# Output projection of an attention layer as seven products of 512-wide blocks in place of eight

## Chip, core and metric

The kernel runs on one core of a Trainium2 chip. The metric is the device time in microseconds (us) of one execution, as the median of several. The engines are TensorE (PE for matmuls, PEld for the loads of their stationary operand), VectorE (DVE), ScalarE (ACT), GpSimd (POOL) and SyncE (SP), which only issues DMAs here.

## What is computed

One layer over a sequence of 1024 rows of width 1024: adaLN, an input projection, two groups of eight attention heads of width 64, each head gated by SiLU, an output projection, a gated residual and a layer norm.

```python
y_fox = _from_heads(fox_out) * silu(fg)          # forgetting attention
y_sb  = _from_heads(sb_out) * silu(sg)           # stick-breaking attention
y = concatenate([y_fox, y_sb], -1) @ w_out       # (1024 x 1024) @ (1024 x 1024)
x = layer_norm(ALPHA * x + gate * y, ln_g, ln_b)
```

All is in float32. The kernel splits both operands of a product into a rounded part ("hi", type fp32r) and the rest ("lo") and sums three products, hi x hi, lo x hi and hi x lo, in PSUM.

## The kernel before

Heads are handled in eight pairs: pairs 0 to 3 are stick-breaking, 4 to 7 forgetting (the layout puts the rows of w_out in that order). A unit is one head of a pair and 128 queries (`order`, L983); 128 units run one after another. For a unit TensorE makes the scores (`att_scores`, L414), ACT, DVE and POOL make the weights; two units later TensorE transposes them (`att_transpose`, L465), and when two neighbours are there it multiplies with the values (`att_pv`, L486): the product is gated on POOL (L514) and stored to DRAM in `y_dr` (L522), that of pair 7 split on the spot into `y7h` and `y7l` (L519, L520).

The order on TensorE is written out by hand (`manual_schedule`, L806); the order on the other engines and in the DMA queues comes from the framework's scheduler, which may put their work well ahead of its place in the text. Between the units `fill` (L978) lets TensorE do steps of the projections of later pairs (`gen_m`, L294; `gen_v`, L342). Their weights come through two raw buffers (`raw_tile`, L113) and are split by `fetch_w` (L119) into a ring of five pairs of tiles (`ring_w`, L116).

Beside the projections of pairs 4 to 7 runs `gen_split_out` (L825): sixteen times it fetches 128 x 512 of w_out, multiplies by the gate (L123), splits (L125, L126) and stores both parts to `wo_dr` (L830, L831), and then lets SPACE = 5 steps pass. During the last projection (`gen_last_g`, L944) the places of u are set free one by one, and `load_wo` (L818) fills them with the split w_out, 512 KB each.

From the fifth unit of pair 7 on, `TAIL` (L973) asks for 2, later 4 and 8 steps of the output projection a unit; the rest follows after the last unit. A step is `o_step` (L871): three matmuls (L882 to L884) of 128 rows (t), one pair, and 512 columns. Rows are taken in `OUT_ORDER`, late ones first, as pair 7 finishes them; `load_y` (L855) fetches and splits the other pairs' values for a row tile on POOL (L862, L863). `o_half` (L888) adds the residual (L897) and takes statistics (L899); after the second half DVE applies gain and bias (L910, L912), read from SBUF (`lngb`) at first, and from PSUM (`ps_gain`, `ps_bias`) after `ln_to_psum`.

## Time and profile before

| | us |
|---|---|
| runs, median of 3 (lowest, highest) | 685.15 (684.91, 685.39) |
| span of the profiled execution | 683.5 |
| matmuls end, from the span's start | 676.7 |
| DMA moved over the span | 81.60 MB |

The profiled execution is listed by its span, from the first to the last instruction; what lies around the span is not shown, and the median stands 1.65 us above it. Times in rows count from the span's start. A matmul's row shows when it starts and how long it is in the pipeline; neighbours overlap, so the distance between starts is what one costs. Idle time of an engine that is not the bottleneck costs nothing.

### The profile page before, as it was taken

Reading aid. Unit: us, or ns where it says so; the run is one execution under the profiler, and the core shown is the slowest. Engines: PE = TensorE matmul, PEld = TensorE weight load, DVE = VectorE, ACT = ScalarE, POOL = GpSimd, SP = SyncE. Lnnn points to the kernel's source line nnn. Section 1 sums busy time; section 2 is a strip of 40 time slices with the busy share of each in tenths; the row PEclk is TensorE's granted clock in tenths of the full one; section 3 lists DMA queues with packets and bytes.
Section 4 is the critical chain, followed back from the end, with each engine's and each line's share of the span. In section 5 each row is a group of like instructions: output and inputs, shape, how many; then the busy total and the mean of one; then the engine's idle time right before and its main releaser. Section 6 shows DMA issues by size and latency. Waiting matters only on the chain.

```text
span 683.5 us, 11770 instructions
## 1 busy us (share of the span) xinstructions
PE 667.2 (98%) x4021; PEld 587.2 (86%) x4021; DVE 450.6 (66%) x914; ACT 382.0 (56%) x861; POOL 427.7 (63%) x558
## 2 busy tenths in 40 slices
PE   5999999999999999999999999999999999999995
PEld 4789898888998888889988888899988889888885
DVE  6785368867666667676675665765566677774645
ACT  5668357856567666566675564655565667531000
POOL 5558977756348566556388896877584364665411
PEclk9999999999999999999999999999999999999999
DMA  9966231112102121122144563453341298143301
GB/s 338 410 236 233 82 105 44 41 29 60 29 9 86 27 57 54 37 55 55 55 131 136 172 176 121 143 166 129 101 150 40 72 327 318 58 162 118 123 31 62
DMA packets 45036, 81.60 MB, mean 119 GB/s; under 512 B 5232, under 2 KB 18864, under 8 KB 44976
## 3 DMA queue, kind: packets, MB, share of 16 engines
q1 hardware_dynamic: 43536, 76.63, 33.8%
q10 hardware_dynamic: 1440, 4.21, 2.2%
q8 instruction: 32, 0.52, 0.3%
q14 instruction: 28, 0.23, 0.1%
HBM read 60.34 MB, written 16.29 MB: 112 GB/s over the span
## 4 chain that ended last, share of the span: by engine, by line
PE 94%; DMA 3%; DVE 2%; ACT 0%; issue 0%; POOL 0%; DVEq 0%
PE m L270 10%; PE m L272 10%; PE m L271 10%; PE pv L493 10%; PE T L478 9%; PE S L428 5%; PE S L427 5%; PE o L884 4%; PE o L882 4%; PE o L883 4%; PE v L327 4%; PE v L328 4%; PE v L329 4%; DMA raws<-in_w_qkg_dram 2%; PE st_late L589 1%; PE st_q L589 1%
## 5 line engine op out<-in xcount | busy, mean ns | idle before, releaser
L270 PE MATMUL m<-uh,whi 128*128 128x512 f32 x304 | 126.4, 416 | 0.0
L272 PE MATMUL m<-uh,wlo 128*128 128x512 f32 x304 | 119.7, 394 | 0.0
L271 PE MATMUL m<-ul,whi 128*128 128x512 f32 x304 | 119.7, 394 | 0.0
L481 DVE TENSOR_TENSOR pt<-T,pt 128x512 fp32r<-128x512 f32 (+2 forms) x192 | 100.5, 550 | 17.5 <-ACT pt L480 16.5
L461 POOL TENSOR_TENSOR be<-be,kp 128x127 f32<-128x127 f32 (+3 forms) x64 | 77.2, 1207 | 33.1 <-DVE kp L457 23.5
L480 ACT CAST pt<-T 128x512 fp32r<-128x512 f32 (+2 forms) x192 | 85.8, 480 | 16.1 <-PE T L478 12.5
L453 DVE TENSOR_TENSOR_SCAN kp<-kp,floor 128x512 f32<-128x512 f32 (+2 forms) x64 | 65.2, 1018 | 31.2 <-ACT kp L447 30.1
L493 PEld LDWEIGHTS pv<-pt,v 128*128 128x128 f32 (+1 forms) x640 | 77.1, 163 | 4.4 <-DVE pt L481 0.7
L493 PE MATMUL pv<-pt,v 128*128 128x256 f32 (+3 forms) x640 | 80.4, 271 | 0.5 <-DVE pt L481 0.5
L442 POOL TENSOR_SCALAR a<-a,l 128x1024 f32<-128x1024 f32 (+3 forms) x64 | 48.1, 751 | 40.3 <-DVE l L441 26.7
L272 PEld LDWEIGHTS m<-uh,wlo 128*128 128x128 f32 x304 | 57.1, 188 | 13.6
L440 ACT ACTIVATE a<-a,nm 128x1024 f32<-128x1024 f32 (+3 forms) x64 | 49.8, 778 | 33.8 <-DVE nm L434 32.7
L427 PE MATMUL S<-k,q 128*128 128x512 f32 (+5 forms) x192 | 66.5, 348 | 0.2 <-DVE nm L434 0.2
L428 PE MATMUL S<-kl,qz 128*128 128x512 f32 (+5 forms) x192 | 65.5, 342 | 0.0
L270 PEld LDWEIGHTS m<-uh,whi 128*128 128x128 f32 x304 | 57.3, 188 | 8.5 <-DVE kl L258 0.2
L271 PEld LDWEIGHTS m<-ul,whi 128*128 128x128 f32 x304 | 57.4, 189 | 8.0
L434 DVE CUSTOM_DVE_ANT_0 a<-S,fb 128x1024 f32<-128x1024 f32 (+3 forms) x64 | 48.3, 755 | 20.1 <-PE S L428 9.3
L514 POOL TENSOR_TENSOR ty<-ty,sg 64x256 f32<-64x256 f32 x64 | 47.5, 742 | 22.3 <-DVE ty L513 11.1
L447 ACT ACTIVATE kp<-S 128x128 f32<-128x128 f32 (+3 forms) x64 | 41.7, 652 | 31.6 <-PE S L428 29.4
L327 PE MATMUL v<-whi_v,uh 128*128 128x256 f32 (+1 forms) x192 | 56.0, 292 | 0.0
L405 ACT CAST qz<-q 64x128 fp32r<-64x128 f32 x128 | 37.4, 295 | 33.2 <-PE S L428 31.8
L328 PE MATMUL v<-whi_v,ul 128*128 128x256 f32 (+1 forms) x192 | 54.2, 282 | 0.0
(285 smaller groups left out, 1593.6 us busy)
## 6 DMA issues: line engine op xcount, KB each, us to landing
raw<-in_w_qkg_dram SPq DMA_DIRECT2D x38, 256.0 KB, 2.9
wss<-in_w_ss_dram SPq DMA_DIRECT2D x16, 512.0 KB, 8.4
x<-in_x_dram SPq DMA_DIRECT2D x8, 512.0 KB, 6.9
k<-k SPq DMA_DIRECT2D x32, 128.0 KB, 2.3
wg<-in_w_gate_dram SPq DMA_DIRECT2D x8, 512.0 KB, 4.9
raw_o<-in_w_out_dram SPq DMA_DIRECT2D x16, 256.0 KB, 2.8
fb<-f_dr ACTq DMA_DIRECT2D x8, 512.0 KB, 4.3
wo_dr<-whi_o SPq DMA_DIRECT2D x16, 256.0 KB, 2.5
```

Of the source, the lines that this page charges most:

```text
L270: nc.tensor.matmul(acc, hi[:, c], u_hi[kt][:, s], start=(kt == 0), stop=False)
L271: nc.tensor.matmul(acc, hi[:, c], u_lo[kt][:, s], start=False, stop=False)
L272: nc.tensor.matmul(acc, lo[:, c], u_hi[kt][:, s], start=False, stop=(kt == NB - 1))
L327: nc.tensor.matmul(acc[:, :n], u_hi[kt][:, ts_], hi[:, s], start=(kt == 0), stop=False)
L328: nc.tensor.matmul(acc[:, :n], u_lo[kt][:, ts_], hi[:, s], start=False, stop=False)
L427: nc.tensor.matmul(S[:, s, :w], qst[p][h][:, qs], kst[p][h][:, ks], start=True, stop=False)
L428: nc.tensor.matmul(S[:, s, :w], z, klo[p][:, ks], start=False, stop=True)
L453: scan = nc.vector.tensor_tensor_scan(rv, rv, floor[0][:, 512 - n:][:, ::-1], initial=0.0, op0=ALU.mult, op1=ALU.max)
L461: nc.gpsimd.tensor_tensor(be[:, :ke - 1], be[:, :ke - 1], kp[:, 1:ke], op=ALU.mult)
L480: nc.scalar.copy(hi[:, :n, qo:qo + P], t3)
L481: nc.vector.tensor_tensor(lo[:, :n, qo:qo + P], t3, hi.bitcast(F32)[:, :n, qo:qo + P], op=ALU.subtract)
L493: nc.tensor.matmul(acc[:m, q0:256], vt[p][:, kb, h * P:h * P + m], pt[:, kb % 4, q0:], start=start, stop=stop)
```

## The change

Y (rows x heads) and W (heads x columns) are cut into four blocks of 512 x 512. Y's A11, A12 are rows 0 to 511 (LOW) of pairs 0 to 3 and 4 to 7, A21 and A22 are rows 512 to 1023 (HIGH); B11, B12, B21, B22 likewise. In place of eight block products there are seven: S1 = A21 + A22, S2 = S1 - A11, S3 = A11 - A21, S4 = A12 - S2; T1 = B12 - B11, T2 = B22 - T1, T3 = B22 - B12, T4 = B21 - T2 (the code stores it so); p1 = A11 B11, p2 = A12 B21, p3 = S4 B22, p4 = A22 T4, p5 = S1 T1, p6 = S2 T2, p7 = S3 T3. The four result blocks are sums of these products, which DVE adds. `gen_split_out` makes and stores all seven weight blocks, with a partial sum held in one of the two raw buffers. All heads' values go to `y_dr`, and `PREP` and the generators load them back in blocks of 512 rows, add on POOL, and split. The lower four row tiles get p7, p6, p4 and p5 and are finished by `lower_done` (ACT, POOL); the upper four are started with p1, p6 and p5, and finished with p2 and p3 in `gen_last`. `y_a11`, `y_a22` and `y_s1` load one block and split it as the others do; `upper_done` is the old `o_half`'s end, `load_rows` and `load_upper` fetch x.

```diff
-    SPACE = 5
+    SPACE = 3
...
-    wo_dr = dr.tile([2, NPAIR, P, D], F32, tag="wo_dr", name="wo_dr")
+    OPS = ("B11", "T3", "T2", "T4", "T1", "B21", "B22")
+    wo_dr = dr.tile([len(OPS), 2, 2, P, D], F32, tag="wo_dr", name="wo_dr")
+    s_dr = dr.tile([2, 4, P, 512], F32, tag="s_dr", name="s_dr")
...
-        if p == NPAIR - 1:
...
-            nc.scalar.copy(yh[r, qs], yt[r, :])
-            nc.gpsimd.tensor_tensor(yl[r, qs], yt[r, :], yh.bitcast(F32)[r, qs], op=ALU.subtract)
-        else:
-            nc.sync.dma_start(y_dr[p, r, qs], yt[r, :])
+        nc.sync.dma_start(y_dr[p, r, qs], yt[r, :])
...
+    def load_op(name, jp, tags):
...
+            nc.sync.dma_start(t.bitcast(F32), wo_dr[o, x_, jp])
...
     def gen_split_out():
-        for pr in range(NPAIR):
-            for h in range(2):
-                s = slice(h * 512, h * 512 + 512)
-                hi, lo = fetch_w(f"o{pr}_{h}", w_out[pr * P:(pr + 1) * P, s], 512, gate[:, s])
-                nc.sync.dma_start(wo_dr[0, pr, :, s], hi.bitcast(F32)[:, :512])
-                nc.sync.dma_start(wo_dr[1, pr, :, s], lo.bitcast(F32)[:, :512])
-                for _ in range(SPACE):
-                    yield
+        def fetch(pr, h, key):
+            s = slice(h * 512, h * 512 + 512)
+            raw = raw_tile(f"raw_o{key}")[:, :512]
+            nc.sync.dma_start(raw, w_out[pr * P:(pr + 1) * P, s])
+            nc.gpsimd.tensor_tensor(raw, raw, gate[:, s], op=ALU.mult)
+            return raw
+        def store(name, j, raw):
+            hi, lo = (t[:, :512] for t in ring_w(f"o{name}{j}"))
+            nc.scalar.copy(hi, raw)
+            nc.gpsimd.tensor_tensor(lo, raw, hi.bitcast(F32), op=ALU.subtract)
+            at = slice(j % 2 * 512, j % 2 * 512 + 512)
+            for x_, t in enumerate((hi, lo)):
+                nc.sync.dma_start(wo_dr[OPS.index(name), x_, j // 2, :, at], t.bitcast(F32))
+        def less(out, a, b):
+            nc.vector.tensor_tensor(out, a, b, op=ALU.subtract)
+            return out
...
+        for j in range(4):
+            cur = fetch(j, 0, f"a{j}")
+            store("B11", j, cur)
+            yield from pause()
+            new = fetch(j, 1, f"b{j}")
+            cur = less(new, new, cur)
+            store("T1", j, cur)
+            yield from pause()
+            new = fetch(4 + j, 1, f"c{j}")
+            store("B22", j, new)
+            cur = less(new, new, cur)
+            store("T2", j, cur)
+            yield from pause()
+            yield from pause()
+            new = fetch(j, 0, f"d{j}")
+            store("T3", j, less(new, cur, new))
+            yield from pause()
+            new = fetch(4 + j, 0, f"e{j}")
+            store("B21", j, new)
+            store("T4", j, less(new, new, cur))
+            yield from pause()
+            yield from pause()
...
+        lgb[0] = [att_tile(f"ln_{x_}") for x_ in "gb"]
+        nc.sync.dma_start(lgb[0][0], ln_g.to_broadcast([P, D]))
+        nc.sync.dma_start(lgb[0][1], ln_b.to_broadcast([P, D]))
...
+    def raw_pair(key, home=None):
+        turns[0] += 1
+        if home is None and turns[0] % 2:
+            home = gate
+        if home is not None:
+            return home[:, LOW], home[:, HIGH]
+        return [raw_tile(f"y{x_}_{key}")[:, :512] for x_ in "ab"]
+    def y_home(name, j):
+        jp, at = j // 2, slice(j % 2 * 512, j % 2 * 512 + 512)
+        if name in ("A11", "A22"):
+            if (name, jp) not in yop:
+                yop[name, jp] = sb.tile([P, 4, 512], F32R, tag="v", bufs=3, name=f"y{name}_{jp}")
+            yop[name, j, "t"] = [yop[name, jp][:, 2 * (j % 2) + x_, :] for x_ in range(2)]
+        elif name in ("S2", "S4"):
+            yop[name, j, "t"] = [t[:, :512] for t in ring_w(f"{name}_{j}")]
         else:
+            tags = {"S3": ("u4", "v4", "u5", "v5"), "S1": ("u4", "v4", "u5", "v5"),
+                    "A12": ("q", "q", "k", "k")}[name][2 * jp:2 * jp + 2]
+            if (name, jp) not in yop:
+                yop[name, jp] = [big(t, 4 if t in "qk" else 1, f"y{name}_{jp}_{x_}", F32R)
+                                 for x_, t in enumerate(tags)]
+            yop[name, j, "t"] = [t[:, at] for t in yop[name, jp]]
+        return yop[name, j, "t"]
+    def y_split(name, j, raw):
+        hi, lo = y_home(name, j)
+        nc.scalar.copy(hi, raw)
+        nc.gpsimd.tensor_tensor(lo, raw, hi.bitcast(F32), op=ALU.subtract)
+    def y_less(out, a, b):
+        nc.gpsimd.tensor_tensor(out, a, b, op=ALU.subtract)
...
+    def y_s3(j):
+        a, b = raw_pair(f"S3{j}")
+        nc.sync.dma_start(a, y_dr[j, :, LOW])
+        nc.sync.dma_start(b, y_dr[j, :, HIGH])
+        y_less(b, a, b)
+        y_split("S3", j, b)
+    def y_s2(j):
+        a, b = raw_pair(f"S2{j}")
+        nc.sync.dma_start(a, y_dr[j, :, HIGH])
+        nc.sync.dma_start(b, y_dr[4 + j, :, HIGH])
+        nc.gpsimd.tensor_tensor(b, a, b, op=ALU.add)
+        nc.sync.dma_start(s_dr[0, j], b)
+        nc.sync.dma_start(a, y_dr[j, :, LOW])
+        y_less(a, b, a)
+        nc.sync.dma_start(s_dr[1, j], a)
+        y_split("S2", j, a)
...
+    def y_s4(j):
+        home = (lambda: big("sg", 2, "y_c0"), lambda: big("kl", 2, "y_c1"), lambda: gate, lambda: None)[j]()
+        a, b = raw_pair(f"S4{j}", home) if home is not None else [raw_tile(f"y{x_}_S4{j}")[:, :512] for x_ in "ab"]
+        nc.sync.dma_start(b, s_dr[1, j])
+        for c in (slice(256, 512), slice(0, 256)) if j == 3 else (LOW,):
+            nc.sync.dma_start(a[:, c], y_dr[4 + j, :, c])
+            (hi, lo), (hi4, lo4) = yop["A12", j, "t"], yop["S4", j, "t"]
+            nc.scalar.copy(hi[:, c], a[:, c])
+            nc.gpsimd.tensor_tensor(lo[:, c], a[:, c], hi.bitcast(F32)[:, c], op=ALU.subtract)
+            y_less(b[:, c], a[:, c], b[:, c])
+            nc.scalar.copy(hi4[:, c], b[:, c])
+            nc.gpsimd.tensor_tensor(lo4[:, c], b[:, c], hi4.bitcast(F32)[:, c], op=ALU.subtract)
+    def block_step(acc, yname, wname, t, j, a=0, b=512):
+        yh, yl = (v[:, t * P:(t + 1) * P] for v in yop[yname, j, "t"])
+        hi, lo = w_of(wname, j, a, b)
+        acc = acc[:, :b - a]
+        nc.tensor.matmul(acc, yh, hi, start=j == 0, stop=False)
+        nc.tensor.matmul(acc, yl, hi, start=False, stop=False)
+        nc.tensor.matmul(acc, yh, lo, start=False, stop=j == 3)
...
+    def add_to(r, s, acc):
+        nc.vector.tensor_tensor(r[:, s], r[:, s], acc, op=ALU.add)
...
+    def lower_done(t):
+        r, row = lower[t], 4 + t
...
+        sums, rs, squares = small("sums"), small("rs"), [pv_tile(f"sq_{x_}_{row}", x_) for x_ in range(2)]
...
+        nc.scalar.activation(r, r, AF.Identity, accum_out=sums[:, 0:1])
+        nc.gpsimd.tensor_scalar(mv[:, 0:1], sums[:, 0:1], -1.0 / D, 1.0, op0=ALU.mult, op1=ALU.mult)
+        for x_, s in enumerate((LOW, HIGH)):
+            nc.scalar.activation(squares[x_], r[:, s], AF.Square, bias=mv[:, 0:1],
+                                 accum_out=(sums[:, 1:2], mv[:, 1:2])[x_])
+        nc.gpsimd.tensor_tensor(rs[:, 0:1], sums[:, 1:2], mv[:, 1:2], op=ALU.add)
+        nc.gpsimd.tensor_scalar(rs[:, 0:1], rs[:, 0:1], 1.0 / D, EPS, op0=ALU.mult, op1=ALU.add)
+        nc.gpsimd.tensor_tensor(rs[:, 0:1], rs[:, 0:1], mhalf, op=ALU.pow)
+        nc.gpsimd.tensor_tensor(rs[:, 1:2], mv[:, 0:1], rs[:, 0:1], op=ALU.mult)
+        nc.scalar.activation(r, r, AF.Identity, scale=rs[:, 0:1], bias=rs[:, 1:2])
+        for s in (LOW, HIGH):
+            nc.gpsimd.tensor_tensor(r[:, s], r[:, s], lgb[0][0][:, s], op=ALU.mult)
+            nc.vector.tensor_tensor(r[:, s], r[:, s], lgb[0][1][:, s], op=ALU.add)
+            nc.sync.dma_start(out[row * P:(row + 1) * P, s], r[:, s])
...
+    def gen_first_half():
+        for p0 in (0, 2):
+            ts = (p0, p0 + 1)
+            accs = {t: acc_tile(f"p1_{t}") for t in ts}
+            for jp in range(2):
+                for t in ts:
+                    for j in (2 * jp, 2 * jp + 1):
+                        block_step(accs[t], "A11", "B11", t, j)
+                        yield
+                    if jp:
+                        if t % 2 == 0:
+                            c1[t // 2] = big(("sg", "kl")[t // 2], 2, f"c1_{t // 2}")
+                        nc.scalar.copy(c1[t // 2][:, t % 2 * 512:][:, :512], accs[t])
+            if p0 == 2:
+                for jp in range(2):
+                    load_op("T4", jp, (("u0", "v0"), ("u1", "v1"))[jp])
+                for j in range(4):
+                    y_a22(j)
+            for t in ts:
+                acc = acc_tile(f"p7_{t}")
+                for j in range(4):
+                    block_step(acc, "S3", "T3", t, j)
+                    yield
+                for s in (LOW, HIGH):
+                    nc.vector.scalar_tensor_tensor(lower[t][:, s], lower[t][:, s], ALPHA, acc,
+                                                   op0=ALU.mult, op1=ALU.add)
+        for jp in range(2):
+            load_op("T1", jp, (("u2", "v2"), ("u3", "v3"))[jp])
+        for j in range(4):
+            y_s1(j)
+    def product(acc, yname, wname, t):
+        for j in range(4):
+            block_step(acc, yname, wname, t, j)
+            yield
+    def gen_second_half():
+        u2 = [pt_tile(x_, f"u2_{x_}", F32, [P, 2, 512]) for x_ in range(2)]
+        for p0 in (0, 2):
+            ts = (p0, p0 + 1)
+            for t in ts:
+                acc = acc_tile(f"p6_{t}")
+                yield from product(acc, "S2", "T2", t)
+                nc.vector.tensor_tensor(u2[t // 2][:, t % 2], c1[t // 2][:, t % 2 * 512:][:, :512], acc, op=ALU.add)
+                for s in (LOW, HIGH):
+                    add_to(lower[t], s, u2[t // 2][:, t % 2])
+            if p0 == 2:
+                for jp in range(2):
+                    load_op("B22", jp, (("u6", "v6"), ("u7", "v7"))[jp])
+                for j in range(4):
+                    y_home("A12", j)
+                    y_home("S4", j)
+                    y_s4(j)
+            for t in ts:
+                acc = acc_tile(f"p4_{t}")
+                yield from product(acc, "A22", "T4", t)
+                add_to(lower[t], LOW, acc)
+            if p0 == 0:
+                load_ln()
+                for t in range(3, -1, -1):
+                    load_upper(t)
+                for jp in range(2):
+                    load_op("B21", jp, ("pth", "ptl"))
+            for t in ts:
+                acc = acc_tile(f"p5_{t}")
+                yield from product(acc, "S1", "T1", t)
+                add_to(lower[t], HIGH, acc)
+                for s, part in ((LOW, c1[t // 2][:, t % 2 * 512:][:, :512]), (HIGH, u2[t // 2][:, t % 2])):
+                    nc.vector.scalar_tensor_tensor(upper[t][:, s], upper[t][:, s], ALPHA, part,
+                                                   op0=ALU.mult, op1=ALU.add)
+                add_to(upper[t], HIGH, acc)
+                lower_done(t)
+        ln_to_psum()
+    def gen_last():
+        for t in range(3, -1, -1):
+            final = t == 0
+            acc = acc_tile(f"p2_{t}")
+            for j in range(4):
+                block_step(acc, "A12", "B21", t, j)
                 yield
+            add_to(upper[t], LOW, acc)
+            groups = ((0, 256), (256, 512)) if final else ((0, 512),)
+            row_stats(upper[t], t, 0, LOW, 1 + len(groups))
...
+            for g, (a, b) in enumerate(groups):
+                acc = acc_tile(f"p3_{t}_{a}")
+                for j in range(4):
+                    block_step(acc, "S4", "B22", t, j, a=a, b=b)
+                    yield
+                s = slice(512 + a, 512 + b)
+                add_to(upper[t], s, acc[:, :b - a])
+                row_stats(upper[t], t, 1 + g, s)
+            upper_done(t)
...
-            load_wo(kt)
+            home = (("B11", 0), ("B11", 1), ("T3", 0), ("T3", 1), None, None, ("T2", 0), ("T2", 1))[kt]
+            if home:
+                load_op(*home, (f"u{kt}", f"v{kt}"))
...
-    YLOAD = (6, 9, 12, 14, 16)
+    PREP = {-4: (y_a11, 0), -2: (y_a11, 1), 2: (y_a11, 2), 3: (y_a11, 3), 4: (y_s3, 0), 5: (y_s3, 1),
+            6: (y_s3, 2), 7: (y_s3, 3), 8: (y_s2, 0), 9: (y_s2, 1), 10: (y_s2, 2), 12: (y_s2, 3)}
...
-    tail = chain([gen_out_first(6), gen_out_last(6)] + [gen_out(t) for t in OUT_ORDER[1:]])
+    tail = chain([gen_first_half(), gen_second_half(), gen_last()])
...
-        if k == LAST:
-            load_y(6)
-            load_ln()
-        for i, d in enumerate(YLOAD):
-            if k == LAST + d:
-                load_y(OUT_ORDER[i + 1])
-    for t in OUT_ORDER[1 + len(YLOAD):]:
-        load_y(t)
-    ln_to_psum()
+        if k - LAST in PREP:
+            prepare, j = PREP[k - LAST]
+            prepare(j)
+        if 3 <= k - LAST < 7:
+            load_rows(k - LAST - 3)
```

155 lines of the change are left out of this document (64 added, 91 removed).

## The prediction, made before the changed kernel ran

> **What bounds the kernel now.** I read the page first (busy shares, then the chain that ended last), and then the table of windows, to see which engine has room in which stage.
>
> ```profile
> span 683.5 us, 11770 instructions
> PE 667.2 (98%) x4021; PEld 587.2 (86%) x4021; DVE 450.6 (66%) x914; ACT 382.0 (56%) x861; POOL 427.7 (63%) x558
> PE 94%; DMA 3%; DVE 2%; ACT 0%; issue 0%; POOL 0%; DVEq 0%
> ```
>
> The chain is TensorE for 94% of the span: taking matmuls away shortens the kernel, as long as what feeds TensorE keeps up. The 63% of POOL is a mean over very different stages. The windows hold PE, PEld, DVE, ACT and POOL busy, then the clock, the DMA share and GB/s.
>
> ```profile
> core 0: us, PE busy (x) PEld busy (x) DVE busy (x) ACT busy (x) POOL busy (x), PEclk, DMA share, GB/s
> 340.00:490.00 150.00, 150.00 (x962) 135.11 (x961) 94.45 (x241) 85.69 (x212) 119.23 (x131) 1.00 0.45 139
> 490.00:560.00 70.00, 69.74 (x399) 59.69 (x397) 46.75 (x122) 42.01 (x103) 40.44 (x50) 1.00 0.44 140
> 560.00:634.50 74.50, 74.50 (x414) 64.02 (x412) 51.72 (x122) 34.18 (x84) 43.02 (x56) 1.00 0.49 176
> 634.50:676.70 42.20, 42.15 (x205) 34.88 (x203) 21.62 (x36) 0.00 (x0) 8.80 (x15) 1.00 0.19 68
> 676.70:683.50 6.80, 0.00 (x0) 0.00 (x0) 3.70 (x8) 0.55 (x1) 1.43 (x3) 0.85 0.21 77
> ```
>
> TensorE is full in every stage up to 676.7. POOL is at 119 of 150 us (79%) where the output weights are split (340 to 490), at 58% beside the last head pair, and nearly idle after 634.5. The change loads just these three places.
>
> **The matmuls removed.** A matmul row lasts 395 ns but overlaps its neighbours, so a matmul costs its distance to the next.
>
> ```profile
> 628.94 0.40 PE L882 MATMUL o<-woh,whi_y 128*128 128x512 f32 x1
> ...
> 634.97 0.39 PE L884 MATMUL o<-wol,whi_y 128*128 128x512 f32 x1
> ```
>
> Between these two starts lie 26 matmuls of 512 columns: 6.03 / 26 = 0.232 us each. Before, the projection is 8 row tiles x 8 pairs x 2 halves x 3 = 384 such matmuls (one half cut in two). After, it is 7 products x 4 row tiles x 4 blocks x 3 = 336. 48 x 0.232 = **11.1 us less**. The closing chain after the last matmul (6.8 us above) keeps its instructions. The loop over the units asks for the same counts of steps (3 x 0.232 = 0.696 us each) as before, 68 in all. Before, 68 are left after it, 16 of them of half width: 52 x 0.696 + 16 x 0.348 = 41.8 us ahead of 676.5, so it ends near 634.7, and it would after the change too, with 48 left. p2 of row tile 3, the first to need A12, then starts at 634.7 + 12 x 0.696 = 643, and p3, which needs S4, asks for its last block near 648.
>
> **The weight sums beside the projections.**
>
> ```profile
> L123 POOL TENSOR_TENSOR raw_o<-raw_o,gate 128x512 f32<-128x512 f32 x15 | 19.5, 1298 | 9.6 <-DMA raw_o<-in_w_out_dram 9.4
> L126 POOL TENSOR_TENSOR wlo_o<-raw_o,whi_o 128x512 fp32r<-128x512 f32 x15 | 19.5, 1298 | 0.7
> L125 POOL TENSOR_SCALAR whi_o<-raw_o 128x512 fp32r<-128x512 f32 x16 | 9.9, 618 | 0.9 <-PE m L271 0.7
> L480 ACT CAST pt<-T 128x512 fp32r<-128x512 f32 x29 | 16.5, 586 | 2.0 <-PE T L478 1.5
> L126 POOL TENSOR_TENSOR wlo<-raw,whi 128x512 fp32r<-128x512 f32 x13 | 16.8, 1295 | 1.3 <-DMA wo_dr<-wlo_o 0.8
> L126 POOL TENSOR_TENSOR wlo_v<-raw_v,whi_v 128x512 fp32r<-128x512 f32 x4 | 5.2, 1296 | 0.3
> raw_o<-in_w_out_dram SPq DMA_DIRECT2D x16, 256.0 KB, 2.8
> L121 SPq DMA_DIRECT2D raw_o<-in_w_out_dram x16: 328/333/577, 314.6 to 475.5; - x16
> L126 POOL TENSOR_TENSOR wlo_o<-raw_o,whi_o x16: 1283/1296/1316, 346.1 to 490.0; 128x512 fp32r<-128x512 f32 x16
> ```
>
> POOL before: 16 x (1.298 + 0.618 + 1.298) = 51.4 us. After: 20 gate products and 28 low parts, 48 x 1.298 = 62.3: 10.9 more, with which the stage stands at 130 of 150 (87%). ACT gains 28 casts, 16.4 us by L480's 586 ns; DVE 16 subtractions, 12 us by 0.75 (L912 below). None of these engines gets full. What is tight is the two raw buffers: a partial sum holds one of them through 15 of the 21 pauses of a round, and the other serves everything else. By these rows four fetches of a round keep it for 4.9 + 6.7 + 6.7 + 8.6 = 27 us, 108 over four rounds; the projections' 17 fetches (13 + 4 above) of 2.8 + 0.62 + 1.30 = 4.7 us add 80. That is 188 us, against the stage's 314.6 to 490 = 175 us x 1.29 (both free for 6 of 21) = 226. It fits at 83%. I take 1 us; the ends are 0 (the projections' matmuls hide it) and 13 us (188 on one buffer alone). The added stores and loads go down SP's queue, with DMA at 0.45 here: no cost.
>
> **The row-side blocks: POOL at the end.** Rows of 560 to 683.5:
>
> ```profile
> L863 POOL TENSOR_TENSOR wlo_y<-yr,whi_y 128x512 fp32r<-128x512 f32 x6 | 7.8, 1301 | 0.4
> L863 POOL TENSOR_TENSOR wlo_y<-yr,whi_y 128x384 fp32r<-128x384 f32 x6 | 6.1, 1017 | 0.5
> L520 POOL TENSOR_TENSOR y7l<-ty,y7h 64x256 fp32r<-64x256 f32 x8 | 5.9, 737 | 2.3 <-ACT y7h L519 2.1
> L176 POOL TENSOR_TENSOR rs_b<-rs_b,mhalf 128x1 f32<-128x1 f32 x7 | 5.4, 771 | 0.6
> L862 POOL TENSOR_SCALAR whi_y<-yr 128x512 fp32r<-128x512 f32 x6 | 3.7, 620 | 1.7 <-PE o L884 0.9 <-POOL ty L514 0.5
> L862 POOL TENSOR_SCALAR whi_y<-yr 128x384 fp32r<-128x384 f32 x6 | 3.1, 515 | 18.7 <-PE o L884 18.7
> L175 POOL TENSOR_SCALAR rs_b<-mv_b 128x1 f32<-128x1 f32 x7 | 2.8, 407 | 13.9 <-DVE mv_b L170 13.6
> ```
>
> Of the 43.0 us of POOL in 560 to 634.5, about 31 go (the y splits 20.7, y7l 5.9, statistics some 4), and 12 of attention stay. Added: 28 low parts and 16 sums, 44 x 1.30 = 57.2, of which two are ready before 560: 54.6. Further lower_done, per row 5 small operations (an estimate of 2.8 us from L175 and L176) and 2 x 1.30: 5.4, two rows of them ahead of 648: 10.8. Together 12 + 54.6 + 10.8 = 77 us in the 88 from 560 to 648. And there is a further claim, on the port:
>
> ```profile
> L910 DVE SCALAR_TENSOR_TENSOR r<-r,mv_b,lngb 128x512 f32<-128x512 f32 x8 | 6.7, 880 | 0.1
> L912 DVE SCALAR_TENSOR_TENSOR r<-r,rs_b,lngb 128x512 f32<-128x512 f32 x8 | 5.9, 747 | 1.5 <-POOL rs_b L176 1.4
> L910 DVE SCALAR_TENSOR_TENSOR r<-r,mv_b,ps_gain 128x512 f32<-128x512 f32 x7 | 5.0, 744 | 0.1
> L176 POOL TENSOR_TENSOR rs_b<-mv_b,mhalf 128x1 f32<-128x1 f32 x1 | 0.6, 569 | 5.2 <-DVE mv_b L170 5.2
> ```
>
> The same DVE operation takes 880 ns with both operands in SBUF and 744 with the gain in PSUM; POOL's power of 128x1 takes 771 beside the first and 569 beside the second. So the two hold each other up. The change gives DVE 20 such operations ahead of 648 (8 sums of u2 into lower rows, 8 starts of upper rows, 4 bias sums). I price POOL's standstill at 0.75 each, 15 us, for POOL is seldom idle there: 92 us in 88. The ends are 0 and 15. The Trainium skill (SBUF — State Buffer, "SBUF: two separate sides") says that a DVE operation with two SBUF inputs and a POOL operation that reads SBUF exclude each other for a whole instruction; the rows above point that way. By that rule the excess stands; without it POOL would have 11 us to spare.
>
> POOL is thus 4 us over if nothing gives way; 4.1 us of the second row's close (2 x 1.30 + 2 x 0.75) may run behind S4. Between 0 and 4, and with idle moments before landings, I take **3 us** of wait, at p2 and p3 of row tile 3; in TensorE's queue every later product stands behind it. lower_done also squares into the banks of pv and fl, so the loop's last pv product waits for row 5's squares: a sum over the row (some 1.1 us), one small POOL operation and a square, about 3 us after p5, beside which p6 of row tile 2 runs for 2.8. I take 0; if POOL is late, it counts among the same 3 us.
>
> **DVE in the last stage.**
>
> ```profile
> L899 DVE BATCH_NORM_STATS2 st_b<-r 128x6 f32<-128x512 f32 x15 | 10.4, 693 | 0.4
> L897 DVE SCALAR_TENSOR_TENSOR r<-xr,o 128x512 f32<-128x512 f32 x15 | 10.2, 686 | 22.6 <-PE o L884 22.5
> ```
>
> Before, a row tile costs DVE 2 x (0.69 + 0.69) + 4 x 0.74 + 0.21 = 5.9 us under 48 x 0.232 = 11.1 us of matmuls; L897 waits 22.5 us for TensorE in all. In gen_last the same work of upper_done stands beside only 24 x 0.232 = 5.6 us. DVE falls behind by 0.3 us a row, starts late by what lower_done's bias sums leave, and the last half finds up to 3 us of the row before in DVE's queue: **1.5 us**, ends 0 and 4.
>
> **The sum** for the profiled execution: 683.5 - 11.1 + 1 + 3 + 1.5 = 677.9. The median of the runs, 685.15, lies 1.65 us above that span; with the same added, **679.5 us**.
>
> **The rivals.**
>
> 1. Everything is hidden, and only the matmuls count: 685.15 - 11.1 = 674.0; without the port's hold-up, but with the 1 and 1.5 above, 676.6. For it: in the plain count POOL has 11 us to spare. Against it: the 880 and 771 ns. Chance 0.20 (up to 677).
>
> 2. The forecast, 677 to 683.8: 0.45.
>
> 3. The waits eat the gain, within 0.2% of before (about what a measurement of this kernel tells from no change): 683.8 to 686.5, when they come to 10 to 12 us: 0.10.
>
> 4. **Slower: the two staging pairs (gate and the raw buffers) that carry S3, S2, A22 and S1 in turn become the chain.**
>
> ```profile
> yr<-y_dr SPq DMA_DIRECT2D x8, 256.0 KB, 3.4
> wol<-wo_dr SPq DMA_DIRECT2D x8, 512.0 KB, 7.7
> 559.73 0.78 PE L493 MATMUL pv<-pt,v 128*128 128x256 f32 x4
> 628.53 0.57 PE L493 MATMUL pv<-pt,v 128*128 128x256 f32 x4
> ```
>
> A11's second half can be split only when pair 6's values are free, after its last pv product at 559.7. From about 564 on each pair carries two blocks of every kind: S3 2 x (2.9 + 1.3 + 0.6 + 1.3), S2 2 x (2.9 + 1.3 + 2.9 + 1.3 + 0.6 + 1.3), A22 and S1 2 x 4.8 each (landing 2.9, an estimate between 2.8 and 3.4): 12.2 + 20.6 + 9.6 + 9.6 = 52 us, so S1 is ready at 616. p5 wants it at 620, twelve steps (8.4 us) ahead of the last pv product at 628.5. Each of a pair's 14 POOL operations may have to wait for what POOL is at: with 0.65 (half of 1.30) 9 us, and S1 comes at 625. With two landings like the 7.7 us under load, 9.6 more, it comes at 634.6, 14.6 us late, in which the 3 us of p2 are contained: 685.15 - 11.1 + 1 + 14.6 + 1.5 = 691.2; with one, 686.4. It decides from 8.6 us of lateness on (11.1 - 1 - 1.5). For it: POOL's 77 to 92 us in 88, and 2.1 MB each of T4, T1, B21 and B22 beside it on the DMA queues. Against it: every block but pair 7's is in DRAM early, and landings of 256 KB took 3.4 us here, the 7.7 us being those of 512 KB in a burst. Chance 0.25.
>
> One row bears on the price of long waits:
>
> ```profile
> 679.00:681.00 2.00, 0.00 (x0) 0.00 (x0) 1.57 (x4) 0.52 (x1) 0.59 (x1) 1.00 0.16 62
> 682.00:683.50 1.50, 0.00 (x0) 0.00 (x0) 0.00 (x0) 0.00 (x0) 0.00 (x0) 0.50 0.04 11
> ```
>
> The granted clock is still 1.00 until 681, 4 us after the last matmul (TensorE is idle from 676.7), and 0.50 from 682: short waits keep it. The Trainium skill (TensorE: Matmul & The Clock Gate, "What's actually happening") puts the window of idleness that halves the clock at about 3.4 us; one wait in a single piece beyond that would by the page cost up to another 3.4 us, which would put the fourth case near 694.
>
> **How the numbers follow.** Faster by over 0.2%: 0.20 + 0.45 = 0.65; same 0.10; slower 0.25. The range, 674.0 to 691.0, goes from the bare count of matmuls to the fourth case's price; some 0.1 lies above (the 13 us of the raw buffers, more long landings), little below, since nothing here removes more than the 48 matmuls. The forecast's own range is 677 to 683.8.
>
> **What would show it.** 336 matmuls' worth of rows in block_step at the same pitch of 0.23; PE idle of some 3 us at p2 and p3 of row tile 3, released by POOL; POOL at 85% or more from 560 to 648; bias and u2 sums on DVE over 0.75 us beside POOL; PE full from 340 to 490. Wrong, if TensorE waits in the projections for whi (raw buffers), at p5 for S1, or nowhere.

## The result and the profile after

The change makes the kernel **slower**: 765.09 us, median of 4 runs (764.07 to 768.32), against 685.27 us (684.91 to 685.41) of the kernel before beside it. The ratio is 1.1175, 95% interval 1.1151 to 1.1199. The forecast was 679.5.

The page of the kernel after: span, busy time of each engine, and the chain that ended last, by engine.

```profile
span 764.3 us, 11991 instructions
PE 684.5 (90%) x3961; PEld 590.3 (77%) x3961; DVE 476.1 (62%) x942; ACT 425.6 (56%) x943; POOL 479.6 (63%) x585
PE 60%; DMA 14%; POOL 12%; DVE 7%; issue 5%; ACT 2%; SPq 0%; POOLq 0%; ACTq 0%; DVEq 0%
```

TensorE was the chain for 94%, now for 60%. POOL is busy for 63% of the span as before, and yet has taken 12% of the chain: that points to its place in a row of waits more than to its load. TensorE's largest waits in the kernel after, from 340 us to the end (total, times, longest):

```profile
PE m L272 <- POOL whi L127: 14.3, 4, 4.8
PE p L978 <- ACT yA L922: 12.8, 2, 10.2
PE v L329 <- POOL whi_v L127: 8.3, 4, 2.8
PE p L978 <- DVE r L993: 6.8, 4, 4.0
PE T L480 <- DVE pt L483: 3.7, 3, 2.2
PE S L429 <- DVE nm L436: 3.3, 3, 1.5
PE m L274 <- POOL wlo L128: 3.3, 3, 2.5
```

The same view of the kernel before has one line for 340 to 683.5:

```profile
PE S L427 <- DVE nm L434: 0.2, 1, 0.2
```

Two groups stand out: projections (m, v) that wait for their split weights, and products of the output projection (p) that wait for a row block (yA) or for VectorE (r). The windows (columns as in the prediction) cut the run where pair 7's last projection (`gen_last_g`) begins, at 600.8 after and 548.4 before; first after, then before:

```profile
340.00:600.90 260.90, 225.98 (x1302) 194.69 (x1301) 142.89 (x358) 136.12 (x326) 164.89 (x168) 0.93 0.41 133
600.90:764.30 163.40, 127.13 (x615) 102.01 (x614) 100.78 (x197) 69.91 (x155) 99.97 (x112) 0.91 0.62 218
```

```profile
340.00:548.40 208.40, 208.14 (x1300) 185.27 (x1299) 132.90 (x341) 121.12 (x295) 151.29 (x170) 1.00 0.42 129
548.40:628.80 80.40, 80.40 (x448) 68.91 (x447) 57.13 (x138) 39.99 (x100) 46.25 (x61) 1.00 0.57 204
628.80:676.40 47.60, 47.60 (x232) 39.49 (x229) 24.50 (x39) 0.77 (x2) 13.96 (x21) 1.00 0.20 70
```

The first stage, that of the weight sums, is 600.8 - 548.4 = **52.4 us later**: TensorE is idle for 34.9 us (0.3 before), and its 1300 matmuls are busy for 17.8 us longer (225.98 against 208.14), at the lower clock. The last stage takes 163.4 us where it took 683.5 - 548.4 = 135.1: **28.3 more**, and 39.4 more than the 124.0 that 11.1 us of removed matmuls would have left. The granted clock has fallen to 0.93 and 0.91.

### The profile page after: what moved, and what is told of

Its sections match the earlier page's. It is cut to its first block, busy times and chain, and to the rows that moved or that the text cites. A ratio compares the mean times of both kernels' runs of the same rounds, so it can differ in the third digit from the quotient of the medians.

```text
span 764.3 us, 11991 instructions
## 1 busy us (share of the span) xinstructions
PE 684.5 (90%) x3961; PEld 590.3 (77%) x3961; DVE 476.1 (62%) x942; ACT 425.6 (56%) x943; POOL 479.6 (63%) x585
## 4 chain that ended last, share of the span: by engine, by line
PE 60%; DMA 14%; POOL 12%; DVE 7%; issue 5%; ACT 2%; SPq 0%; POOLq 0%; ACTq 0%; DVEq 0%
PE m L274 7%; PE m L272 7%; PE m L273 7%; PE pv L493 7%; PE T L480 6%; PE v L331 3%; PE v L329 3%; PE S L430 3%; PE v L330 3%; PE S L429 3%; DMA raws<-in_w_qkg_dram 2%; DMA gate<-s_dr 2%; POOL wlo L128 2%; DMA yb_S<-y_dr 2%; DMA raw<-in_w_qkg_dram 1%
## 5 line engine op out<-in xcount | busy, mean ns | idle before, releaser
L272 PE MATMUL m<-uh,whi 128*128 128x512 f32 x304 | 128.8, 424 | 14.3 <-POOL whi L127 14.3
L274 PE MATMUL m<-uh,wlo 128*128 128x512 f32 x304 | 122.3, 402 | 3.5 <-POOL wlo L128 3.3
L273 PE MATMUL m<-ul,whi 128*128 128x512 f32 x304 | 121.5, 400 | 0.0
L482 ACT CAST pt<-T 128x512 fp32r<-128x512 f32 (+2 forms) x192 | 85.8, 480 | 17.9 <-PE T L480 14.5
L493 PEld LDWEIGHTS pv<-pt,v 128*128 128x128 f32 (+1 forms) x640 | 80.9, 170 | 6.0 <-DVE pt L483 1.1
L493 PE MATMUL pv<-pt,v 128*128 128x256 f32 (+3 forms) x640 | 84.4, 279 | 1.0 <-DVE pt L483 0.8
L444 POOL TENSOR_SCALAR a<-a,l 128x1024 f32<-128x1024 f32 (+3 forms) x64 | 50.4, 788 | 38.6 <-DVE l L443 29.6
L513 DVE TENSOR_TENSOR ty<-pv,ty 64x256 f32<-64x256 f32 x64 | 26.9, 420 | 62.6 <-ACT ty L512 51.6
L331 PE MATMUL v<-wlo_v,uh 128*128 128x256 f32 (+1 forms) x192 | 55.5, 289 | 2.8 <-POOL wlo_v L128 2.8
```

Source lines behind the costliest of these rows:

```text
L272: nc.tensor.matmul(acc, hi[:, c], u_hi[kt][:, s], start=(kt == 0), stop=False)
L273: nc.tensor.matmul(acc, hi[:, c], u_lo[kt][:, s], start=False, stop=False)
L274: nc.tensor.matmul(acc, lo[:, c], u_hi[kt][:, s], start=False, stop=(kt == NB - 1))
L331: nc.tensor.matmul(acc[:, :n], u_hi[kt][:, ts_], lo[:, s], start=False, stop=(kt == NB - 1))
L482: nc.scalar.copy(hi[:, :n, qo:qo + P], t3)
L493: nc.tensor.matmul(acc[:m, q0:256], vt[p][:, kb, h * P:h * P + m], pt[:, kb % 4, q0:], start=start, stop=stop)
```

## The experiments

Each kernel was run once, beside the kernel before (685.05 to 686.16 us on the same chips). The kernel after spreads over 4.3 us in its four runs, so differences of a few us between single times mean little; the start of `gen_last_g` and the rest behind it are read from each kernel's trace. They scatter too: the nine kernels with the same weight sums (after, e4, t_a, t_b, t_c, f1, f2, g1, g2) start between 599.6 and 604.6, and the nine with the same work in the last stage (after, e1, e5, f3, f4, g3, h1, h2, h3) take 161.6 to 165.5 for the rest. Steps under 4 or 5 us below are therefore not clear of the scatter by themselves; they are read beside TensorE's waits in the traces.

| kernel | us | gen_last_g starts | rest of the span |
|---|---|---|---|
| before | 685.27 | 548.4 | 135.1 |
| after | 765.09 | 600.8 | 163.4 |
| e3_before_sums | 735.58 | 598.8 | 135.1 |
| e1_nohold | 732.72 | 565.8 | 165.2 |
| e2_before_hold | 688.18 | 551.4 | 135.1 |
| f4_keep | 753.94 | 589.9 | 162.3 |
| e5_noless | 726.19 | 559.9 | 164.6 |
| f3_16 | 722.96 | 557.1 | 164.1 |
| g3_fetch16 | 720.17 | 556.8 | 161.6 |
| h1_even | 723.37 | 556.1 | 165.5 |
| h2_80 | 720.74 | 554.5 | 164.4 |
| h3_cast | 716.24 | 549.1 | 165.1 |
| e4_order | 768.18 | 602.3 | 164.2 |
| t_c_port | 771.85 | 604.6 | 165.5 |
| t_b_noload | 754.22 | 599.6 | 152.9 |
| t_a_nosums | 749.90 | 602.7 | 145.5 |
| f1_both | 747.19 | 600.5 | 144.9 |
| f2_nolow | 742.95 | 600.6 | 140.3 |
| g1_dve | 738.86 | 602.3 | 134.8 |
| g2_noclose | 735.44 | 599.7 | 134.0 |

Some expectations count these starts from a zero up to 0.6 us apart, and say 11.2, 8.3 and 5.9 for what is 11.5, 8.7 and 6.1 here.

### The two stages apart

e3_before_sums is the kernel before with the new `gen_split_out` alone; its projection loads whatever blocks lie there.

```diff
-        nc.sync.dma_start(hi.bitcast(F32), wo_dr[0, pr])
+        nc.sync.dma_start(hi.bitcast(F32), wo_dr[pr % 7, 0, pr // 4])
```

> The kernel before with the changed gen_split_out (seven blocks, sums held) and the old projection of eight products, whose weights are read from the seven blocks, so the projection is not the reference's. If the weight sums cost what the traces suggest (gen_last_g 51.8 us late) and nothing else of the change does so ahead of pair 7: 685 + 50 = 735. If the late start comes from the row-side work that is put ahead of its place (y_a11 and y_s3 beside the projections): 685 to 700.

It came to 735.58, 50.4 us late at `gen_last_g` and with the old rest of 135.1. The weight sums lose some 50 us by themselves, with nothing of the seven products in the kernel.

### The held raw buffer

```diff
-            cur = less(new, new, cur)
+            cur = less(new, new, new)      # e1, at each of the four sums
```

e1_nohold subtracts a block from itself, so no partial sum lives across the pauses; the work is the same.

> The changed kernel with every subtraction of weight blocks taken within one buffer (new - new in place of new - cur), so that no partial sum is held over the pauses; the number of fetches, products, subtractions and stores stays, the weight sums are not computed. Held-buffer theory: the projections' fetches get both raw buffers back, gen_last_g starts near 550 (600.2 in the changed kernel, 548.4 before), and the time falls by about 50 to some 715. Rival, load theory (the added POOL, DVE and ACT operations and the stores through the ring cost the time, and so does the shared port): gen_last_g stays beyond 585 and the time above 750.

e2_before_hold is the kernel before with the SPACE pauses put between the gate product and the split, so that each raw block is kept through them.

> The kernel before, with the SPACE pauses of gen_split_out moved between the gate product and the split, so that a raw buffer is held through the pauses; nothing is added. Held-buffer theory: the projections' fetches are left with one buffer and the kernel becomes slower by 10 to 50 us. Load theory: within 3 us of before (685).

e1 regains 35.0 of the 52.4 us, and TensorE's waits for split weights (whi, wlo and those of v), 28.7 us ahead of `gen_last_g` in the kernel after, are gone from its trace: the held buffer is the largest cause, though 17.4 us stay that this expectation didn't have. e2 lost 3 us only, a miss, but hardly a test: its trace shows the splits brought forward, 7.7 us behind the gate product on the mean (3.8 before), and at most 3.1 us in seven of the 16 blocks. What holding costs isn't shown by it. Why the buffer costs so much stands in POOL's timeline of the kernel after (start, duration, instruction, in brackets the idle time before it and what ended it):

```profile
404.14 0.62 POOL L127 TENSOR_SCALAR whi<-raw 128x512 fp32r<-128x512 f32 x1 [0.40 <-DMA raw<-in_w_qkg_dram]
408.89 0.62 POOL L127 TENSOR_SCALAR whi<-raw 128x512 fp32r<-128x512 f32 x1 [1.16 <-DMA raw<-in_w_qkg_dram]
414.67 1.29 POOL L831 TENSOR_TENSOR raw_oc<-raw_oc,gate 128x512 f32<-128x512 f32 x1 [2.99 <-DMA raw_oc<-in_w_out_dram]
422.02 1.30 POOL L831 TENSOR_TENSOR raw_od<-raw_od,gate 128x512 f32<-128x512 f32 x1 [0.73 <-DMA raw_od<-in_w_out_dram]
429.86 0.62 POOL L127 TENSOR_SCALAR whi<-raw 128x512 fp32r<-128x512 f32 x1 [2.12 <-DMA raw<-in_w_qkg_dram]
434.46 0.62 POOL L127 TENSOR_SCALAR whi<-raw 128x512 fp32r<-128x512 f32 x1 [2.25 <-DMA raw<-in_w_qkg_dram]
439.35 1.29 POOL L831 TENSOR_TENSOR raw_oe<-raw_oe,gate 128x512 f32<-128x512 f32 x1 [0.95 <-DVE pt L483]
```

The lines show one block after another, never two at a time: 4.6 to 5.8 us from a block to the next, and 7.4 and 7.8 behind the blocks of the sums (raw_oc, raw_od). POOL waits for a DMA before six of the seven, since a fetch can't be issued until the one buffer left is free. When the round's last sum has read the partial sum (VectorE), the next round's first fetch follows at once (SP):

```profile
442.94 0.69 DVE L843 TENSOR_TENSOR raw_oe<-raw_oe,raw_oc 128x512 f32<-128x512 f32 x1
```

```profile
443.66 0.33 SPq L830 DMA_DIRECT2D raw_oa<-in_w_out_dram  x1
```

The freed buffer is taken again within 0.1 us, for the next block that will be held. The same happens at the third change of rounds; at the first, two blocks of a projection come in between. By these two views, a partial sum is held for 232 of the 238 us from the first fetch (314.7) to the last sum (552.8), not for 15 pauses in 21.

f4_keep, the whole computation, writes each partial sum to DRAM and reads it back beside its use:

```diff
+            keep("a", cur)
-            cur = less(new, new, cur)
+            cur = less(new, new, back(f"b{j}"))
```

> The whole computation; nothing is left out. Each partial sum of weight blocks is written to DRAM and read back into a raw buffer beside its use, so that none is held across the pauses: 12 stores and 16 loads of 256 KB more. If the held buffer is what costs 34 us (e1_nohold), the last product of pair 7 starts near 566 to 575, 732 to 742 in all. If the traffic and the second raw buffer, taken for some 3 us at each sum, cost as much as the holding did: above 755.

753.94 lies between the two: `gen_last_g` starts 10.9 us earlier than after, of e1's 35.0. It doesn't separate the holding from the added traffic; as a remedy it is worth a third.

### What stays when nothing is held

Six kernels take further parts away, each from the one before: the subtraction (e5_noless), the sums' splits and stores (f3_16), one fetch of five (g3_fetch16), the uneven spacing (h1_even), a pause more in each round (h2_80), and, further below, the cast on ScalarE (h3_cast).

> As the run without a held sum, and DVE's 16 subtractions of weight blocks are left out too (the seven blocks are then plain blocks of w_out). In that run gen_last_g still started at 565.9, 17.5 late, with TensorE waiting for DVE (pt, nm). Port theory (DVE operations with two SBUF operands and POOL's shut each other out): the lateness falls below 7 and the time to some 720. Load theory (POOL's 10.9 us and ACT's 16.4 us of added work): the lateness stays above 12.

> e5_noless (no held buffer, no subtraction of weight blocks), and the splits and stores of the 12 sums are left out, so that 16 blocks are split as before; the 20 fetches and gate products and the pauses stay, and T1 to T4 are loaded from other blocks. It says what the 11.2 us are by which pair 7's last product still starts late in e5_noless. If it is the load of POOL and ScalarE by 28 splits: late by less than 4 us, about 719. If it is the fetches or their place in the order: still late by more than 8, 723 or more.

> f3_16, and one fetch with its gate product in each round is left out too (16 fetches, as before, in place of 20), the pauses kept. f3_16 starts pair 7's last product 8.3 us later than before. If the added fetches are it: late by less than 3 us, some 717. If it is the order of the pauses (splits closer together): late by 6 or more, 721 or more.

> g3_fetch16 with its 4 fetches of a round (and three splits) spaced evenly, 5 pauses between them as before (one pause more at a round's end: 21 in all), in place of 3, 3, 9 and 6. If the spacing is what makes pair 7's last product 8.4 us late there: late by less than 3 us, near 550, about 714. If not: near 556, about 720.

> h1_even without the one pause more at each round's end: 16 fetches and 80 pauses, as before the change, with 12 splits in place of 16. If the four pauses shift the matmuls beside the attention: late by less than 2 us, near 549, about 713. If 7 us stay late, they don't come from the weight sums' own steps at all but from what else changed ahead of pair 7, about 720.

The subtraction gave 5.9 us (17.4 to 11.5), between e5's two theories. (f3's text has two counts the wrong way round: it leaves out 16 splits and keeps 12, fewer than before.) Then come 2.8, 0.3, 0.7 and 1.6 us, none of them clear of the scatter: no run makes its guess (the splits' load, the fetches, their spacing, the pauses) more than a small part, and 6.1 us are still there, though POOL and the queues now have less to do than before the change. ScalarE's timeline of h2_80 shows what load doesn't:

```profile
386.54 0.62 ACT L836 CAST whi_oB<-raw_oB 128x512 fp32r<-128x512 f32 x1 [4.32 <-POOL raw_oB L831]
387.06 0.58 ACT L243 ACTIVATE q<-m 64x512 fp32r<-64x512 f32 x1
387.55 0.46 ACT L482 CAST pt<-T 128x384 fp32r<-128x384 f32 x1
```

And TensorE's there:

```profile
386.33 0.40 PE L274 MATMUL m<-uh,wlo 128*128 128x512 f32 x1
388.06 0.57 PE L493 MATMUL pv<-pt,v 128*128 128x256 f32 x3 [1.33 <-ACT pt L482]
```

ScalarE stands 4.32 us at the cast of a weight block, which waits for POOL's gate product. The attention's own cast (pt) is behind it in the queue, and TensorE's pv waits for that. Before the change POOL made this cast (L125), so ScalarE's queue had nothing of it.

```diff
-            nc.scalar.copy(hi, raw)
+            nc.gpsimd.tensor_scalar(hi, raw, 1.0, 1.0, op0=ALU.mult, op1=ALU.mult)
```

> h2_80 with the cast of each weight block made by POOL (0.62 us each, 12 of them), as before the change, in place of ScalarE. If the cast waiting in ScalarE's queue holds up the attention: pair 7's last product starts less than 2 us late, near 549, about 715. If not: 5.9 us late, 554, about 721.

Late by 0.7 us: a hit. 12 casts of 0.62 us given back to POOL bring 5.4 us, and TensorE's waits ahead of `gen_last_g` fall from 3.7 to 0.8 us. The windows of h3_cast from 340 up to `gen_last_g` are those of the kernel before again:

```profile
340.00:400.00 60.00, 60.00 (x359) 52.90 (x358) 39.12 (x90) 35.00 (x80) 49.92 (x53) 1.00 0.47 147
400.00:450.00 50.00, 49.35 (x288) 42.72 (x286) 31.00 (x81) 28.17 (x69) 35.15 (x40) 1.00 0.36 107
450.00:548.90 98.90, 98.63 (x658) 89.48 (x657) 62.35 (x170) 58.63 (x149) 58.17 (x67) 1.00 0.37 112
```

The 52.4 us, in this order of taking away: 35.0 held buffer, 5.9 subtraction, 2.8 sums' splits and stores, 2.6 fetches and pauses, 5.4 casts in ScalarE's queue, 0.7 left. Another order would share them out differently; with all 28 splits the casts stand in ScalarE's queue more often.

### The last stage: queue, port, loads, sums

In the kernel after, the longest wait of all is 10.2 us for the row block A22 of p4. SP's queue there:

```profile
674.20 0.38 SPq L877 DMA_DIRECT2D ln_g<-in_ln_g_dram  x1
675.33 0.33 SPq L878 DMA_DIRECT2D ln_b<-in_ln_b_dram  x1
676.03 1.61 SPq L990 DMA_DIRECT2D r<-in_x_dram  x2
678.55 0.33 SPq L953 DMA_DIRECT2D gate<-y_dr  x1
```

ScalarE and TensorE:

```profile
686.74 0.62 ACT L922 CAST yA<-gate 128x512 fp32r<-128x512 f32 x1 [3.59 <-DMA gate<-y_dr]
```

```profile
687.41 0.79 PE L978 MATMUL p<-wT,yA 128*128 128x512 f32 x1 [10.17 <-ACT yA L922]
```

The block of 256 KB was issued behind gain, bias and two row tiles of x, none of them due yet, and landed 686.74 - 678.55 = 8.2 us later. Through the wait, from 677 to 686.7, the DMA share is 1.00 to 1.08, while POOL is busy for 2.2 us. So e4_order makes the loads that aren't due wait for A22 and S1.

```diff
+        with after(marks["a22"]):
             load_op("T1", ...)
+        with after(marks["s1"]):
             load_ln(), load_upper(t), load_op("B21", ...)
```

> The changed kernel with the loads of T1 issued behind A22's last block, and those of ln, x, B21, B22 and S4 behind S1's last block in SP's queue. Queue theory: the 10.8 us wait of p4 for A22 (its block landed 8.2 us after its issue, behind 512 KB loads) shrinks to under 4, and the time falls by 5 to 15 us, to 750 to 760. POOL theory (the blocks are late because POOL has too much to do): within 3 us of 765, or slower since the other loads come later.

A miss: the rest is 164.2. Its longest waits are 6.9 us for A22, 3.7 for S1 and 3.4 for u: the wait of 10.2 became shorter, and others came up. t_c_port leaves VectorE's two-SBUF additions off the port (two groups read PSUM, the bias sum is left out):

```diff
-                    add_to(lower[t], s, u2[t // 2][:, t % 2])
+                    add_to(lower[t], s, acc)
```

> The changed kernel with DVE's sums in the last stage reading PSUM and one SBUF operand (the accumulator in place of c1 and u2; the eight bias sums of lower_done are left out), so the result is not the reference's. Port theory: POOL and DVE are each relieved of some 15 us of standing, the last stage is no more bound by DVE, and the stretch of 163.4 becomes shorter by more than 10. DMA theory: by 3 to 8, at the end alone (the DVE work left out is in the closing chain).

The rest is 165.5, no shorter (2.1 more is within the scatter): for the port theory a miss, but a weak one, since these operations may now hold PSUM accumulators longer. t_b_noload uses blocks again that are in SBUF, in place of loading T4, T1, B21 and B22 (8.4 MB); t_a_nosums leaves the 16 sums of row blocks out.

```diff
-                    load_op("T4", jp, (("u0", "v0"), ("u1", "v1"))[jp])
+                    wop["T4", jp] = wop["B11", jp]          # t_b, four such
-        nc.gpsimd.tensor_tensor(out, a, b, op=ALU.subtract)
+        pass                                                # t_a
```

> The changed kernel without the loads of T4, T1, B21 and B22 (8.4 MB of the last stage); their products use the blocks B11, T3 and T2 that are there, so the result is not the reference's. DMA theory: the waits for A22 and S1 shrink to under 4 in all and the stretch of 163.4 becomes shorter by more than 12. POOL theory: less than 6.

> The changed kernel without the 16 sums of value blocks on POOL (20.8 us); every DMA stays, the sums S1 to S4 are not formed. The changed kernel takes 163.4 us from the start of gen_last_g to its end, 39 more than the matmul count asks for. POOL theory: that stretch becomes shorter by more than 12. DMA theory (blocks land late behind 512 KB loads) and port theory: shorter by less than 6.

The sums are worth 17.9 us of 20.8 us of POOL work (16 x 1.30), the loads 10.5. Are these two costs or one?

> Left out in the last stage: all 16 sums of row blocks (t_a_nosums) and the loads of the weight blocks T4, T1, B21 and B22 (t_b_noload). From the start of pair 7's last product to the end the changed kernel took 163.4 us, 145.5 without the sums, 152.8 without the loads. Separate causes: the gains add, 163.4 - 17.9 - 10.6 = 134.9 us, about 736.5 in all. One wait that either of them can end: at most the larger gain, above 142 us and 743. Matmuls alone would be 135.1 - 11.1 = 124.0.

One: both together give 18.5, a miss for the sum of 28.4. TensorE's waits for row blocks (yA, yS, whi_S, wlo_S) are 18.3 us in the kernel after, 7.8 without the loads, 0.2 without the sums, and none without both. A block's chain (S2's is the longest: landing, sum, store, landing, sum, cast, low part) runs through two staging pairs, and shortening either link brings it nearer to its time. What is next?

> f1_both, and the low parts of all 28 row blocks are left out too (the high part stands in for them), so that POOL has only the attention, the small statistics and the closes of lower rows in the last stage. If POOL's elementwise work and the loads are all that holds the matmuls, the stage takes near 124.0 us (135.1 - 11.1), about 726 in all; then the 11.1 us of the prediction are there. If over 131 us remain, something else (VectorE's sums, the order of the products, the clock) costs more than what the prediction gave it.

> f2_nolow, and 24 of VectorE's operations of the last stage are left out: the 8 additions of u2 into lower rows, the 8 starts of upper rows and the 8 bias sums of the closes (0.69 to 0.96 us each, some 19 us). f2_nolow took 140.3 us from pair 7's last product to the end, VectorE 32.5 of the 38.0 us behind the last pv. If VectorE's queue is the next limit: 128 us or less, some 729 in all. If it is the order of the products or the attention: over 135.

> g1_dve, and the closes of the four lower rows are left out altogether (sum, squares, power, scaling; the sums of products are stored as they are), so that ScalarE and POOL have none of it. What stays is the matmuls, their evacuation, the attention and the upper rows' closes. If the matmul term of the prediction holds: 124 to 126 us from pair 7's last product to the end, 725 to 727 in all. If over 130 us remain, the 11.1 us of matmuls are not there.

Without low parts 4.6 us less, without 24 of VectorE's operations (19 us) another 5.5, without the closes 0.8. The first two are little more than the scatter, but TensorE's waits for VectorE's additions of products (into r) shrink with them: 8.3 us in f1_both, 4.1 in f2_nolow, 1.3 in g1_dve. The expectations' floors (124 to 128) were not reached. The windows of g2_noclose, cut at `gen_last_g`, the last pv product and the last matmul of the projection:

```profile
599.70:689.00 89.30, 82.79 (x447) 69.77 (x447) 48.65 (x126) 51.71 (x120) 20.11 (x28) 0.98 0.75 265
689.00:725.00 36.00, 36.00 (x171) 29.89 (x170) 22.08 (x36) 2.73 (x6) 3.12 (x7) 1.00 0.18 65
725.00:733.70 8.70, 0.30 (x3) 0.10 (x1) 5.60 (x13) 0.55 (x1) 1.63 (x4) 0.82 0.32 121
```

Against 80.4, 47.6 and 7.1 before: behind the last pv TensorE is full, and 11.6 us are gone (the end has 1.6 more). There the removed matmuls show. Ahead of it 8.9 us are lost at the same number of matmuls, beginning with this wait of TensorE:

```profile
614.49 0.37 PE L430 MATMUL S<-kl,qz 128*128 128x448 f32 x1
617.03 1.25 PE L480 MATMUL T<-ident,a 128*128 128x128 f32 x7 [2.18 <-DVE pt L483]
```

DVE's half of pt follows ScalarE's, and ScalarE's timeline there reads:

```profile
612.87 0.60 ACT L922 CAST yS<-yb_S 128x512 fp32r<-128x512 f32 x1
613.50 0.36 ACT L512 COPY ty<-pv 64x256 f32<-64x256 f32 x1
613.89 0.62 ACT L922 CAST yA<-gate 128x512 fp32r<-128x512 f32 x1
614.41 0.61 ACT L922 CAST yA<-ya_A 128x512 fp32r<-128x512 f32 x1
614.93 1.06 ACT L482 CAST pt<-T 128x512 fp32r<-128x512 f32 x2
```

The attention's cast (pt) comes behind three casts of row blocks. By the pattern of h3_cast that is again a cost of ScalarE's queue, but moving these casts wasn't tried: argued, not shown. None of the runs points to a version that beats the kernel before.

## Why the prediction was wrong, by its own steps

- **The matmuls removed** (11.1 us): right, but visible only when all that feeds them was taken away (11.6 in g2_noclose).
- **The weight sums** (1 us, ends 0 and 13): the step that failed first and most, with 52.4. "It fits at 83%" rested on two numbers that do not hold. One is "both free for 6 of 21", the pauses of the text: the text on the kernel itself says that the scheduler may put such work well ahead of its place, it did, and a partial sum was held for 232 of 238 us. With that nearly the whole stage goes by one buffer. The other is "314.6 to 490.0 = 175 us": the second fetch of w_out came at 346.2 only (345.9 after the change), as the prediction's own row of L126 shows, whose first low part starts at 346.1. The "188 on one buffer alone" had 490 - 346 = 144 us, and would have been 44 over, not 13 (an estimate from these rows); so even the term's upper end was too low. The uses also lasted longer than the prediction's rows gave (7.4 and 7.8 us from block to block where it had 6.7), and half the clock behind the waits made the matmuls longer by 17.8 us, which it had at nothing.
- "None of these engines gets full" was true (ACT 136 of 261 us) and didn't help: 12 casts moved into ScalarE's in-order queue cost 5.4 us by waiting there. The prediction counted their 586 ns and not what was queued behind them. The subtraction, priced as 12 us on an engine with room, cost 5.9.
- **POOL at the end** (3 us, ends 0 and 4): it was sized as a load, "92 us in 88". POOL was busy 99.97 of 163.4 us (61%) and late all the same. The sums cost 17.9 us as links of a chain: with them go 18.1 of the 18.3 us that TensorE waits for row blocks, and POOL stood idle for most of the longest of these waits.
- **The port**: the hold-up is there, and larger than priced for one operation. VectorE's groups in the kernel after, from 560 on, by shape: sums with a PSUM operand (p) and with two in SBUF (u, ln_b):

```profile
L993 DVE TENSOR_TENSOR r<-r,p 128x512 f32<-128x512 f32 x19 | 12.6, 680 | 17.4 <-PE p L980 17.3
L993 DVE TENSOR_TENSOR r<-r,u 128x512 f32<-128x512 f32 x8 | 8.4, 1084 | 0.1
L1022 DVE TENSOR_TENSOR r<-r,ln_b 128x512 f32<-128x512 f32 x8 | 9.7, 1231 | 0.5 <-POOL r L1021 0.5
```

  In f2_nolow, with little left on POOL, the same two take 824 and 815 ns. This agrees with the exclusion that the Trainium skill states (SBUF — State Buffer, "SBUF: two separate sides"). As a cause of the end time it stays open: t_c_port was no clean test.
- **DVE in the last stage** (1.5 us, ends 0 and 4): at the very end the mechanism and the size were right. The last matmul starts 9.1 us before the end of the span, 7.1 before the change; the 2.0 us are the last half standing behind the row before (L1033) in VectorE's queue. From the chain that ended last in the kernel after:

```profile
756.30 0.41 DVE r L993
756.71 1.32 DVE r L1033 x2
758.03 0.35 DVE st_b L1000
```

  Ahead of that VectorE costs more: g1_dve puts it at 5.5 once POOL's work is gone. The starts of upper rows and the sums of u2 stand in its queue among the evacuations that free the accumulators; the prediction counted only the upper closes.
- **The fourth rival** had the right mechanism: the staging pairs as the chain, with a landing under load (8.2 us measured, 7.7 assumed). The price of the waits was near (18.3 us for row blocks where it had 14.6), the place was not: 14.4 of them are for A22 at p4, 2.4 for S1 at p5. With the waits for VectorE and the lower clock the stage loses 39.4. Its chance of 0.25 looks too low, for the argument against it (256 KB landed in 3.4 us) took a row from a quiet queue.
- "Wrong, if TensorE waits in the projections for whi (raw buffers), at p5 for S1": both waits are there.
- **"Short waits keep" the clock**: wrong; see the last section.

## What to carry to other kernels

A buffer kept across a pause must be priced as if it were held all the time, unless the order of the work is fixed: here the next use was issued as soon as the buffer came free. And the time that a buffer has is counted from when its uses can follow each other, not from the first of them. Work moved to an engine with room still costs what waits behind it in that engine's queue, and a chain through DMA, POOL and ScalarE can be late by its length while POOL and ScalarE have room. Before a saving in matmuls is counted, the time of every operand that feeds them has to be laid out against the moment that it is due, with landings taken from rows under load.

## What the runs showed of the hardware

The granted clock halves after a wait of 2.18 us already, though behind the last matmul of the kernel before it stayed at 1.00 for 4 us. The length of the wait alone doesn't decide it: in the kernel after, TensorE waited 2.22 us up to 420.07, and the clock was 1.00 from 419 to 426. g2_noclose, around the wait quoted above, in windows of 1 us:

```profile
616.00:617.00 1.00, 0.00 (x0) 0.00 (x0) 1.00 (x5) 0.95 (x2) 0.00 (x0) 1.00 1.01 399
617.00:618.00 1.00, 0.97 (x8) 0.82 (x8) 0.65 (x2) 0.78 (x3) 0.13 (x1) 0.94 1.05 406
618.00:619.00 1.00, 1.00 (x5) 0.81 (x4) 0.68 (x2) 0.97 (x3) 0.88 (x1) 0.50 1.01 387
...
621.00:622.00 1.00, 1.00 (x6) 0.96 (x5) 0.07 (x1) 0.11 (x1) 0.00 (x0) 0.85 0.52 135
```

The half clock comes after TensorE is back at work, and lasts some 3.4 us (0.94, three windows of 0.50, 0.85). A matmul of 512 columns is 0.43 us behind the last there in place of 0.23, so a wait of 2.2 us can cost up to 1.6 more. The Trainium skill (TensorE: Matmul & The Clock Gate, "What's actually happening") has half the clock after an idle window of about 3.4 us; the length of the stretch agrees, the wait that it takes was shorter here.
